# Later values for the large attention units, two gates ahead of the last values, and scores in four PSUM banks

## The chip, the cores and the metric

The kernel runs on one core of a Trainium2 chip. The metric is the device time of one execution in microseconds (us). Lower is better. Six queues of work appear in the profile: PE (TensorE matmuls), PEld (its weight loads), DVE (VectorE), ACT (ScalarE), POOL (GpSimd) and SP (SyncE, which issues the DMAs here).

## The reference

A trunk of two layers over 512 tokens of width 1024. In a layer, x is normalised and projected by one wide matrix into all inputs of two branches. One branch (NSA) has 8 query heads in 2 groups and adds three attentions per head, each with its own gate: over compressed keys, over selected blocks of keys, over a window. With 512 tokens, 8 blocks of 64 and a window of 512, the selection takes every block and the window every earlier token, so the second and the third are plain causal attentions over two sets of keys. The other branch (GLA) is a gated linear attention in chunks of 64. Then

```
y   = sigmoid(p_mg_nsa) * (o_nsa @ w_up_nsa) + sigmoid(p_mg_gla) * (o_gla @ w_up_gla)
out = x + rms(y @ w_out) * g_post
```

## The kernel before

**Precision and weights.** Large products are made of three fp32r matmuls: each operand is split in a rounded part and a rest (`H`, `Lo`), and `split3` adds H·H, H·Lo, Lo·H. Weights come in a fixed order (`ORDER`) through SP into `raw` (3 buffers). ACT makes H (L145) and DVE makes Lo (L146), both into the pool `hl`, whose 6 buffers hold three weights. `get` asks for the weights two places ahead.

**Order of the work.** PE's instructions run in the order in which the program writes them. ACT, DVE, POOL and SP get their order from a planner at build time, which works with its own estimates. Projections are generators in a `queue`: `fill(us)` lets about so many microseconds of queued matmuls out on PE, `need(name)` runs the queue until `name` is done. So the projections of the layer (`q`, `nz`, then for f = 0..7 the gate `mgg` and the up-projection `ug` of the GLA branch) are spread between the steps of the attention.

**The attention.** Heads are worked in four pairs p (heads p and p+4). A pair has five units, so there are 20 units n, with m = n % 5:

- m = 0 is the compressed attention, in three steps: scores into a bank of pool `s`, then softmax; PE transposes of the weights into a bank of pool `t` (L755), which ACT reads (L757) and then DVE (L758); and the product with the compressed values (L761, L762), which opens the pair's accumulator, the only bank of pool `o`.
- m = 1, 2 are the small units (first 256 tokens, key sets 0 and 1). m = 3, 4 are the large units (last 256 tokens, key sets 0 and 1). Each has three steps: `scores` for its first block of 128 tokens, `scores` for its second, and the values (L840), 32 matmuls in each pair of large units, which add to the accumulator. One call of `scores` (at m = 1 it serves both key sets) takes two PSUM banks, one for each head, and PE fills them in that order (L799). DVE reads them (L812), ACT takes the exponential (L814), DVE scales (L816, L817) and transposes in blocks (L778). The result goes out to DRAM (`tp<-T`, L783) and back in another layout (`PT<-tp`, L786). The values read that copy.

`go(n)` runs the next step of unit n. After the last values of a pair the accumulator is scaled by DVE (L845), rounded by ACT (L847), and the rest is made by POOL (L848); that is `oTn[p]`.

**PSUM.** Eight banks: 3 in `mm` (projections), 2 in `s`, 2 in `t`, 1 in `o`.

**After the attention.** For f = 0..7, `up` makes a gate projection `mgn` (24 matmuls) and an up-projection `un` (12 matmuls) over `oTn[0..3]`, three matmuls for each k.

```
        for n in range(len(steps) + 3):
            m = n % 5
            ...
            go(n)
            if m == 2:
                go(n - 4)
                go(n - 3)
```

These two calls are the values of the large units of the pair before. For the last pair they come in the loop's last round, n = 22.

Of the kernel before, what the change touches and what calls it, by code (L numbers as in the profile page):

```python
# [19 lines left out]
KT = D // 128  # L20
# [39 lines left out]
FILL = [(1.6, 1.6, 1.6, 1.6), (1.0, 0.7, 0.9, 1.0), (1.2, 1.0, 1.0, 1.0), (1.5, 1.2, 1.5, 1.8), (1.3, 1.0, 1.0, 1.0)]  # L60
# [4 lines left out]
def trunk(ctx, tc, x, wpk, sp, gvec, cs, wa, out):  # L65
# [23 lines left out]
    def new(pl, shape=(128, 512), dt=F32, tag=None, bufs=None):  # L89
        cnt[0] += 1  # L90
        kw = {} if bufs is None else {"bufs": bufs}
        return sb[pl].tile(list(shape), dt, tag=tag or pl, name=f"{tag or pl}_{cnt[0]}", **kw)

    def ps(tag):
        cnt[0] += 1
        return psp[tag].tile([128, 512], F32, tag=tag, name=f"ps_{tag}_{cnt[0]}")
# [57 lines left out]
    def get(l, n, ahead=2):  # L154
        issue(POS[l, n] + ahead)
        return ready.pop((l, n))

    def split3(o, w, h, first, last):

        mm(o, w[0], h[0], start=first, stop=False)  # L160
        mm(o, w[0], h[1], start=False, stop=False)  # L161
        mm(o, w[1], h[0], start=False, stop=last)  # L162

    def fm(l, n, hT, then):

        w = get(l, n)
        o = ps("mm")
        for k in range(KT):
            if type(w) is list:
                wk = [t[:, k % 4 * 128:(k % 4 + 1) * 128] for t in w[k // 4]]  # L170
            else:
                wk = [t[:, k * 128:(k + 1) * 128] for t in w]
            split3(o, wk, hT(k), k == 0, k == KT - 1)
            if k == KT - 1:
                then(o)
            yield 0.64
# [94 lines left out]
    for l in range(L):  # L271
# [15 lines left out]
        def put(name, gen):  # L287
            queue.append((name, gen))
# [3 lines left out]
        def fill(us):  # L292
            credit[0] += us
            while credit[0] > 0.3 and queue:
                credit[0] -= step(*queue[0])

        def step(name, gen):
            try:
                return next(gen)
            except StopIteration:  # L300
                queue.pop(0)
                done.add(name)
                return 0.0

        def need(name):
            while name not in done:
                step(*queue[0])
# [78 lines left out]
        for t in range(2):  # L386
            o = ps("s")
# [186 lines left out]
        def up(f, gate, wn, src, then):  # L574
            th = []

            def sig(o):
                th.append(new("th"))
                A.activation(th[0], o, AF.Tanh, scale=0.5)

            yield from fm(l, f"{gate}{f}", hT, sig)
            w = get(l, f"{wn}{f}")
            u = ps("mm")
            for k in range(4):
                sl = slice(k * 128, (k + 1) * 128)
                split3(u, (w[0][:, sl], w[1][:, sl]), src[k], k == 0, k == 3)
                if k == 3:
                    then(th[0], u)
                yield 0.64
# [138 lines left out]
        oTn = [None] * 4  # L728
# [33 lines left out]
            mm(acc, vbd[1], pcT, start=False, stop=False, skip_group_check=True)  # L762
            yield

        PT, TT, held, back = {}, {}, {}, []

        def turn(p, br, i, pps):

            ip, n = i // 2, i + 1
            r = (4 * ip + 3) * 64
            if i % 2 == 0:
                TT[p, br] = new("T", (128, 4, r), tag=f"T{ip}")
            T = TT[p, br]
            t = T[:, :, (i % 2) * i * 64:((i % 2) * i + n) * 64].rearrange("p b (j g q) -> p b j g q", j=n, g=2)
            for g in range(2):
                V.transpose(t[:, :, :, g], pps[g][:, :n * 128].rearrange("p (j b q) -> p b j q", j=n, b=4))  # L778
            if i % 2:
                cnt[0] += 1  # L780
                dr = dram.tile([128, 4, r], F32, tag=f"tp{ip}", name=f"tp_{cnt[0]}", bufs=2)
                with tc.issue_after(back[-1]) if back else nullcontext():
                    dma(dr, T)  # L783
                W = PT[p, br, ip] = new("PT", (128, 4, r), tag=f"PT{ip}")
                for b in range(4):
                    back.append(dma(W[b * 32:(b + 1) * 32], dr[:, b].rearrange("(a k) r -> k a r", a=4)).ins)  # L786

        def scores(p, i, brs):

            w = (i + 1) * 128
            ww = w * len(brs)
            both = len(brs) > 1
            o = [ps("s"), ps("s")]
            for g in range(2):
                for n in range(2):
                    kn = first[g][:, n].rearrange("p b n -> p (b n)") if both else keys[brs[0]][g][n][:, :w]
                    mm(o[g][:, :ww], PR[p][1][g][:, i * 128:(i + 1) * 128], kn, start=(n == 0), stop=(n == 1))  # L799
            pps = [weigh(p, g, i, brs, o[g]) for g in range(2)]  # L800
            turn(p, brs[0], i, [t[0] for t in pps])
            if both:
                held[p] = [t[1] for t in pps]

        def weigh(p, g, i, brs, o):
            h, w = p + 4 * g, (i + 1) * 128
            out = []
            for n, br in enumerate(brs):
                ob = o[:, n * w:(n + 1) * w]
                sx = new("sm", (128, 4), tag="sx", bufs=8)  # L810
                pp = new("g")
                V.tensor_tensor_reduce(pp[:, :w], ob, cmask[:, 512 - w:512], 1.0, -3 * NEG,  # L812
                                       OP.add, OP.min, sx[:, 0:1])
                A.activation(pp[:, :w], pp[:, :w], AF.Exp, bias=sx[:, 0:1], scale=-1.0,  # L814
                             accum_out=sx[:, 1:2])
                V.reciprocal(sx[:, 2:3], sx[:, 1:2])  # L816
                V.tensor_scalar(pp[:, :w], pp[:, :w], sx[:, 2:3],  # L817
                                gt[:, i, h * 3 + 1 + br:h * 3 + 2 + br], op0=OP.mult, op1=OP.mult)
                out.append(pp)
            return out  # L820
# [31 lines left out]
        steps = []  # L852
# [5 lines left out]
        def go(n):  # L858
            if 0 <= n < len(steps):
                next(live[n])  # L860


        for n in range(len(steps) + 3):
            m = n % 5
            f4 = FILL[m]
            if n < len(steps):
                if m == 0:
                    need(f"q{steps[n][0]}")
                if m == 4:
                    need(f"nz{steps[n][0]}")  # L870
            go(n)
            if m == 2:
                go(n - 4)
                go(n - 3)
            fill(f4[0])
            if m == 1:
                go(n - 1)
            fill(f4[1])
            if m != 0:
                go(n)  # L880
                fill(f4[2])
            if m == 2:
                go(n - 2)
            if m == 4:
                go(n - 3)
                go(n - 2)
            fill(f4[3])
        need("ug7")

        yT = []  # L890

        def take_un(f):
            def g(th, u):
                t_ = new("p")
                V.scalar_tensor_tensor(t_, th, 1.0, u, op0=OP.add, op1=OP.mult)  # L895
                G.tensor_tensor(t_, t_, y2[f], op=OP.add)  # L896
                if f < 3:
                    both = new("PT", (128, 2, 512), F32R, tag="PT1") if f < 2 else new("T", (128, 2, 512), F32R, tag="T1")
                    H, Lo = both[:, 0], both[:, 1]
                else:  # L900
                    H, Lo = new("g", dt=F32R), new("g", dt=F32R)
                A.mul(H, t_, 0.5)
                V.scalar_tensor_tensor(Lo, t_, 0.5, H.bitcast(F32), op0=OP.mult, op1=OP.subtract)
                yT.append((H, Lo))
            return g

        for f in range(8):
            put(f"un{f}", up(f, "mgn", "un", oTn, take_un(f)))
        need("un7")


# [7 lines left out]
        for s in range(ST):  # L919
# [4 lines left out]
            o = [ps("s" if s % 2 and n < 2 else "mm") for n in range(len(pieces))]  # L924
# [100 lines left out]
```

## Time and profile before

| | |
|---|---|
| median of 3 runs | 850.48 us (849.61 to 852.71) |
| profiled execution, own time | 847.07 us |
| its span in the profile | 845.0 us |
| PE busy | 792.1 us, 94% |
| DVE busy | 560.0 us, 66% |
| ACT, POOL busy | 352.7 us, 94.6 us |

The span lies 2.07 us below the execution's own time. PE is the busiest engine by far. A matmul of 512 columns is listed with some 0.39 us because matmuls overlap, and the next one starts about 0.23 us later, so the busy share is not the share of its peak. Bracketed numbers at the end of a timeline row are the time in which the engine stood idle before that row, and who ended it.

### The profile page before, as it was taken

To read this page: it belongs to the slowest core of one execution; us is meant where nothing else is said; L and a number is where in the kernel's file an instruction comes from. 1 tells how busy PE (TensorE), PEld (TensorE's weight loads), DVE (VectorE), ACT (ScalarE), POOL (GpSimd) and SP (SyncE) were. 2 spreads that over 40 slices of the span, in tenths; PEclk is the share of its full clock that TensorE was granted. 3 is DMA by queue.
4 is the path that set the end of the run, shared out by engine and by line. 5 is a ranking of instruction groups with operands and counts; after the bars stand their busy time and mean duration, and the time that the engine had idled before them with its cause. 6 is when DMAs were issued, how large, how long until landed. Compare 5 with 4: busy or idle time off the path is not lost. (4 is left out here: it accounts for less than half of the span.)

```text
span 845.0 us, 11999 instructions
## 1 busy us (share of the span) xinstructions
PE 792.1 (94%) x4250; PEld 647.3 (77%) x4250; DVE 560.0 (66%) x1272; ACT 352.7 (42%) x727; POOL 94.6 (11%) x118
## 2 busy tenths in 40 slices
PE   3999999999999969999999999998898999799996
PEld 3888788777777748888898878886686777588886
DVE  5653748998978845555564375788987978275322
ACT  4681236554534423442256313555452545154311
POOL 3100023011000001121010001400000000112100
PEclk9999999999999989999999999999999999899999
DMA  8532124367657483546245121434857677355322
GB/s 286 164 125 86 51 67 122 105 183 224 213 165 237 142 233 91 183 138 209 85 136 203 51 75 51 115 91 142 232 175 206 188 206 221 108 152 163 98 100 74
DMA packets 54555, 124.55 MB, mean 147 GB/s; under 512 B 6592, under 2 KB 23520, under 8 KB 54496
## 3 DMA queue, kind: packets, MB, share of 16 engines
q1 hardware_dynamic: 54496, 123.79, 47.5%
q8 instruction: 33, 0.54, 0.3%
q14 instruction: 26, 0.21, 0.1%
HBM read 95.46 MB, written 25.17 MB: 143 GB/s over the span
## 5 line engine op out<-in xcount | busy, mean ns | idle before, releaser
L160 PE MATMUL ps_mm<-hT,hl 128*128 128x512 f32 x544 | 218.9, 402 | 0.0
L161 PE MATMUL ps_mm<-hT,hl 128*128 128x512 f32 x544 | 213.1, 392 | 0.0
L162 PE MATMUL ps_mm<-hT,hl 128*128 128x512 f32 x544 | 212.7, 391 | 0.0
L146 DVE TENSOR_TENSOR hl<-raw,hl 128x1024 fp32r<-128x1024 f32 (+3 forms) x109 | 126.6, 1163 | 48.5 <-ACT hl L145 46.3
L145 ACT CAST hl<-raw 128x1024 fp32r<-128x1024 f32 (+3 forms) x110 | 100.0, 912 | 135.0 <-PE ps_mm L161 95.8
L160 PEld LDWEIGHTS ps_mm<-hT,hl 128*128 128x128 f32 x544 | 102.7, 189 | 24.3 <-issue 4.4
L162 PEld LDWEIGHTS ps_mm<-hT,hl 128*128 128x128 f32 x544 | 102.6, 189 | 22.4
L161 PEld LDWEIGHTS ps_mm<-hT,hl 128*128 128x128 f32 x544 | 102.9, 189 | 18.9
L814 ACT ACTIVATE g<-g,sx 128x128 f32<-128x128 f32 (+3 forms) x128 | 71.1, 556 | 91.7 <-DVE sx L812 90.1
L778 DVE STREAM_TRANSPOSE T<-g 128x256 f32<-128x256 f32 (+3 forms) x128 | 61.2, 497 | 13.2 <-DMA tp<-T 12.6
L812 DVE CUSTOM_DVE_ANT_0 g<-ps_s,cmask 128x128 f32<-128x128 f32 (+3 forms) x128 | 58.2, 476 | 8.4 <-PE ps_s L799 8.1
L840 PE MATMUL ps_o<-PT,a 128*64 128x256 f32 (+1 forms) x384 | 42.9, 368 | 21.3 <-DMA PT<-tp 21.3
L817 DVE TENSOR_SCALAR g<-g,sx,gt 128x128 f32<-128x128 f32 (+3 forms) x128 | 56.6, 454 | 0.9
L840 PEld LDWEIGHTS ps_o<-PT,a 128*64 128x64 f32 x384 | 27.8, 144 | 38.0 <-issue 26.3
L799 PE MATMUL ps_s<-a,a 128*128 128x256 f32 (+2 forms) x224 | 48.3, 334 | 4.9 <-DVE sx L812 4.8
L161 PE MATMUL ps_mm<-oT,hl 128*128 128x512 f32 x128 | 50.0, 391 | 0.0
L160 PE MATMUL ps_mm<-oT,hl 128*128 128x512 f32 x128 | 50.0, 390 | 0.0
L162 PE MATMUL ps_mm<-oT,hl 128*128 128x512 f32 x128 | 49.8, 389 | 0.0
L799 PEld LDWEIGHTS ps_s<-a,a 128*128 128x128 f32 x224 | 37.7, 188 | 13.0 <-DVE sx L812 7.7
L848 POOL TENSOR_TENSOR oT<-p,oT 128x512 fp32r<-128x512 f32 x8 | 10.4, 1296 | 248.1 <-ACT oT L847 248.1
L183 POOL TENSOR_TENSOR rs<-ms,mhalf 128x1 f32<-128x1 f32 (+1 forms) x24 | 18.0, 751 | 174.2 <-DVE ms L181 170.6
L896 POOL TENSOR_TENSOR p<-p,g 128x512 f32<-128x512 f32 x16 | 25.4, 1589 | 107.7 <-DVE p L895 96.2
(250 smaller groups left out, 1263.3 us busy)
## 6 DMA issues: line engine op xcount, KB each, us to landing
raw<-wpk SPq DMA_DIRECT2D x96, 512.0 KB, 3.8
tp<-T SPq DMA_DIRECT2D x16, 896.0 KB, 4.5
PT<-tp SPq DMA_DIRECT2D x64, 224.0 KB, 4.8
raw<-wpk SPq DMA_DIRECT2D x32, 256.0 KB, 3.2
tp<-T SPq DMA_DIRECT2D x16, 384.0 KB, 2.6
PT<-tp SPq DMA_DIRECT2D x64, 96.0 KB, 2.2
a<-wpk SPq DMA_DIRECT2D x16, 256.0 KB, 4.4
p<-x SPq DMA_DIRECT2D x16, 256.0 KB, 2.7
```

What stands on the lines that cost most here:

```text
L145: A.copy(H[:, :w], r[:, :w])
L146: (G if i == 1 else V).tensor_tensor(Lo[:, :w], r[:, :w], H[:, :w].bitcast(F32), op=OP.subtract)
L160: mm(o, w[0], h[0], start=first, stop=False)
L161: mm(o, w[0], h[1], start=False, stop=False)
L162: mm(o, w[1], h[0], start=False, stop=last)
L778: V.transpose(t[:, :, :, g], pps[g][:, :n * 128].rearrange("p (j b q) -> p b j q", j=n, b=4))
L799: mm(o[g][:, :ww], PR[p][1][g][:, i * 128:(i + 1) * 128], kn, start=(n == 0), stop=(n == 1))
L812: V.tensor_tensor_reduce(pp[:, :w], ob, cmask[:, 512 - w:512], 1.0, -3 * NEG, OP.add, OP.min, sx[:, 0:1])
L814: A.activation(pp[:, :w], pp[:, :w], AF.Exp, bias=sx[:, 0:1], scale=-1.0, accum_out=sx[:, 1:2])
L817: V.tensor_scalar(pp[:, :w], pp[:, :w], sx[:, 2:3], gt[:, i, h * 3 + 1 + br:h * 3 + 2 + br], op0=OP.mult, op1=OP.mult)
L840: mm(acc[g * 64:(g + 1) * 64, (i0 + 2) * 128 - w:(i0 + 2) * 128], vsw[j // 2][:, j % 2, c0:c0 + 64], m, start=False, stop=(br == 1 and j = ...
L896: G.tensor_tensor(t_, t_, y2[f], op=OP.add)
```

## The change

Three edits, in the attention of each layer.

1. The values of the large units of a pair move from m = 2 of the next pair to its m = 3. The product that opens the next accumulator moves with them, from m = 2 to m = 3.
2. The loop ends after 20 rounds. For the last pair, the rest of the queue is run first, then the gate projections `mgn0` and `mgn1`, then the values of units 18 and 19, then the rest of `un0`, `un1` and the others.
3. Successive calls of `scores` take their two banks from `s` and `t` in turn, by a counter `nsc` that starts at 0 in each layer. A pair has seven such calls. The transposes L755 stay in `t` and the compressed scores in `s`.

```diff
-        PT, TT, held, back = {}, {}, {}, []
+        PT, TT, held, back, nsc = {}, {}, {}, [], [0]
...
-            o = [ps("s"), ps("s")]
+            nsc[0] += 1
+            o = [ps("ts"[nsc[0] % 2]) for _ in range(2)]
...
-        for n in range(len(steps) + 3):
+        for n in range(len(steps)):
             m = n % 5
             f4 = FILL[m]
...
             go(n)
-            if m == 2:
-                go(n - 4)
-                go(n - 3)
+            if m == 3:
+                go(n - 5)
+                go(n - 4)
             fill(f4[0])
             if m == 1:
                 go(n - 1)
             fill(f4[1])
             if m != 0:
                 go(n)
                 fill(f4[2])
-            if m == 2:
-                go(n - 2)
+            if m == 3:
+                go(n - 3)
             if m == 4:
                 go(n - 3)
                 go(n - 2)
             fill(f4[3])
         need("ug7")
+
+        uns = [up(f, "mgn", "un", oTn, take_un(f)) for f in range(8)]
+        for f in range(2):
+            for k in range(KT):
+                next(uns[f])
+        go(len(steps) - 2)
+        go(len(steps) - 1)
         for f in range(8):
-            put(f"un{f}", up(f, "mgn", "un", oTn, take_un(f)))
+            put(f"un{f}", uns[f])
         need("un7")
```

## Rows read from the trace of the kernel before

**Rows 1.** The page: busy time of each engine over the span

```profile
PE 792.1 (94%) x4250; PEld 647.3 (77%) x4250; DVE 560.0 (66%) x1272; ACT 352.7 (42%) x727; POOL 94.6 (11%) x118
```

**Rows 2.** Waits of PE, whole span: total us, times, longest

```profile
PE ps_o L840 <- DMA PT<-tp: 21.3, 8, 6.6
...
PE ps_s L799 <- DVE sx L812: 4.8, 4, 1.9
PE ps_t L755 <- DVE g L751: 2.7, 3, 0.9
PE ps_t L755 <- ACT g L814: 1.9, 1, 1.9
```

**Rows 3.** Timeline of PE: values of large units, end of the attention

```profile
237.84 1.73 PE L840 MATMUL ps_o<-PT,a 128*64 128x256 f32 x16 [1.84 <-DMA PT<-tp]
...
305.20 1.74 PE L840 MATMUL ps_o<-PT,a 128*64 128x256 f32 x16
313.49 3.20 PE L840 MATMUL ps_o<-PT,a 128*64 128x256 f32 x16 [6.55 <-DMA PT<-tp]
316.62 0.50 PE L160 MATMUL ps_mm<-hT,hl 128*128 128x512 f32 x1
...
322.23 0.39 PE L160 MATMUL ps_mm<-oT,hl 128*128 128x512 f32 x1
322.46 0.39 PE L161 MATMUL ps_mm<-oT,hl 128*128 128x512 f32 x1
...
725.37 3.25 PE L840 MATMUL ps_o<-PT,a 128*64 128x256 f32 x16 [6.33 <-DMA PT<-tp]
```

**Rows 4.** Windows of layer 0: the four pairs, and the very last values

```profile
core 0: us, PE busy (x) PEld busy (x) DVE busy (x) ACT busy (x) POOL busy (x), PEclk, DMA share, GB/s
147.60:181.00 33.40, 30.73 (x148) 24.89 (x146) 32.15 (x94) 18.39 (x45) 2.59 (x2) 1.00 0.38 118
181.00:219.50 38.50, 36.67 (x200) 29.28 (x199) 34.55 (x102) 18.30 (x48) 3.56 (x2) 1.00 0.71 206
219.50:258.20 38.70, 35.97 (x197) 28.71 (x196) 32.50 (x101) 18.24 (x45) 1.30 (x1) 1.00 0.66 201
258.20:296.00 37.80, 36.66 (x200) 29.27 (x199) 31.45 (x97) 16.61 (x44) 1.30 (x1) 1.00 0.65 192
...
313.49:316.69 3.20, 3.20 (x17) 1.97 (x17) 0.00 (x0) 0.00 (x0) 0.00 (x0) 0.53 0.02 5
```

**Rows 5.** Timeline of SP's queue, end of the attention in layer 0

```profile
298.06 1.74 SPq L786 DMA_DIRECT2D PT<-tp  x4
302.36 0.34 SPq L783 DMA_DIRECT2D tp<-T  x1
302.80 1.33 SPq L132 DMA_DIRECT2D raw<-wpk  x2
306.97 1.75 SPq L786 DMA_DIRECT2D PT<-tp  x4
```

**Rows 6.** Timelines of DVE, ACT and POOL, end of the attention

```profile
306.21 1.22 DVE L146 TENSOR_TENSOR hl<-raw,hl 128x1024 fp32r<-128x1024 f32 x1
316.72 0.69 DVE L845 SCALAR_TENSOR_TENSOR p<-ps_o,oT 128x512 f32<-128x512 f32 x1 [9.29 <-PE ps_o L840]
322.90 0.69 DVE L146 TENSOR_TENSOR hl<-raw,hl 128x512 fp32r<-128x512 f32 x1 [5.49 <-ACT hl L145]
...
317.45 0.62 ACT L847 CAST oT<-p 128x512 fp32r<-128x512 f32 x1 [11.28 <-DVE p L845]
...
318.15 1.29 POOL L848 TENSOR_TENSOR oT<-p,oT 128x512 fp32r<-128x512 f32 x1 [35.58 <-ACT oT L847]
```

**Rows 7.** Timeline around L755 and L758, pairs 0 and 2, layer 0

```profile
155.34 0.60 PE L755 MATMUL ps_t<-ident,g 128*64 128x128 f32 x4
156.48 0.63 PE L799 MATMUL ps_s<-a,a 128*128 128x256 f32 x4
157.22 0.58 ACT L757 CAST p<-ps_t 64x512 fp32r<-64x512 f32 x1
159.65 0.68 DVE L758 TENSOR_TENSOR p<-ps_t,p 64x512 fp32r<-64x512 f32 x1
166.62 0.62 PE L799 MATMUL ps_s<-a,a 128*128 128x384 f32 x2 [1.94 <-DVE sx L812]
...
231.65 0.64 PE L799 MATMUL ps_s<-a,a 128*128 128x256 f32 x4
232.72 0.69 DVE L758 TENSOR_TENSOR p<-ps_t,p 64x512 fp32r<-64x512 f32 x1
```

More of the change, by code (lines that the diff above doesn't have):

```diff
@@ L860, in go @@
                 next(live[n])
-        for n in range(len(steps) + 3):
[L864 to L871, printed above, removed]
-            if m == 2:
-                go(n - 4)
-                go(n - 3)
[L875 to L881, printed above, removed]
-            if m == 2:
-                go(n - 2)
[L884 to L888, printed above, removed]
         yT = []
@@ L905, in take_un @@
             return g
+        for n in range(len(steps)):
+            m = n % 5
+            f4 = FILL[m]
+            if m == 0:
+                need(f"q{steps[n][0]}")
+            if m == 4:
+                need(f"nz{steps[n][0]}")
+            go(n)
+            if m == 3:
+                go(n - 5)
+                go(n - 4)
+            fill(f4[0])
+            if m == 1:
+                go(n - 1)
+            fill(f4[1])
+            if m != 0:
+                go(n)
+                fill(f4[2])
+            if m == 3:
+                go(n - 3)
+            if m == 4:
+                go(n - 3)
+                go(n - 2)
+            fill(f4[3])
+        need("ug7")
+        uns = [up(f, "mgn", "un", oTn, take_un(f)) for f in range(8)]
[4 more added lines that the diff above has]
+        go(len(steps) - 1)
         for f in range(8):
-            put(f"un{f}", up(f, "mgn", "un", oTn, take_un(f)))
+            put(f"un{f}", uns[f])
         need("un7")
```

## The prediction

> **What bounds the kernel now.** First the page: PE is busy 94% of the span, the next engine, DVE, 66% [rows 1]. So what PE waits for is what can be won, and work that leaves another engine wins nothing by itself. Then the waits of PE. The largest entry is the values' matmuls waiting for the copy that comes back from DRAM: 21.3 us in 8 waits. Behind it stand 4.8 us in which scores wait for DVE to empty their bank, and 2.7 + 1.9 us in which the transposes L755 wait for the softmax [rows 2]. All three lie in the attention, and the change touches each.
>
> Then the timeline, to see which of the eight waits weigh. In each layer one stands at the very end of the attention: 6.55 us in layer 0, 6.33 us in layer 1 [rows 3]. That is 12.9 us. The other six share 21.3 − 12.9 = 8.4 us. The one shown, at 237.84, is the largest with 1.84 us, and it belongs, as the others do, to the large units of a pair whose values come at m = 2 of the next.
>
> The long waits have a second price. After 6.55 us without work the 16 matmuls of unit 19 take 3.20 us, where the 16 of unit 18 before the wait took 1.74 us [rows 3]. The granted clock of that stretch is 0.53, the lower of the two levels (1.2 of 2.4 GHz) for nearly all of it, where the pairs ahead show 1.00 [rows 4].
>
> SP's queue shows why the end waits. The last block's transposes go out at 302.36, the copy back is issued at 306.97, and PE goes on at 313.49 [rows 5, 3]: 11.1 us for the way through DRAM. The queue of projections ran dry before that: from 305.20 on PE has only values, and the matmuls that follow at 316.62 are already `mgn0` [rows 3]. So the loop's last round finds nothing to put in front of them.
>
> **The end of the attention (edit 2).** It adds no work. It puts `mgn0` and `mgn1` ahead of the two last values. One gate is 24 matmuls, from 316.62 to 322.23: 5.6 us [rows 3]. The GLA work ends at 305.20, as before. The two gates end at 305.2 + 11.2 = 316.4, unit 18 at 318.1, and unit 19 needs a copy that has landed by 313.5. That leaves 4.6 us to spare, so the whole wait goes, and with it the slow clock: 6.55 + 1.46 in layer 0, 6.33 + 1.51 in layer 1, in sum −15.85 us.
>
> Can the gates run that early? The rest of `mgn1` is made by 307.43 [rows 6], and it is wanted at 310.8. `un1` takes the buffers that `mgn0` frees: before, the weight of 512 columns followed the end of a gate at 322.23 by 1.4 us (its rest is done at 323.59 [rows 6]), so it is ready at some 312.2. It is wanted after `un0`, not before 319.8 + 12 × 0.23 = 322.6. `get` now asks for `mgn2` earlier, one 512 KB load further up in SP's queue, but no copy of the attention is issued after it.
>
> What is late next is `oTn[3]`. Before, the 5.6 us of `mgn0` hid it. Now only `un0` stands behind the last values. From the end of unit 19 (313.49 + 3.20 = 316.69) DVE, ACT and POOL need until 319.44, that is 2.75 us [rows 6]. PE has nine matmuls over the first three heads and one on the rounded part of the fourth before it needs the rest: 10 × 0.23 = 2.3 us [rows 3]. So it waits 0.45 us, and behind it waits all of PE. If one rest of 1.22 us [rows 6] stands before it on DVE it is 1.7 us. I take 0.5, twice: +1.0 us, with 0 and +3.4 as bounds.
>
> **Values a step later (edit 1).** The same 32 matmuls, later by the fills of m = 2, nominally 1.2 + 1.0 + 1.0 + 1.0 = 4.2 us of projections, and by the scores of a block. The six waits are at most 1.84 us, so the copies have landed. −8.4 us. The accumulator is freed later too, but the product that opens the next one is moved behind it by the same step, and before its place come two fills of 1.5 and 1.2 us, where the scaling of the old one takes 0.69 us [rows 6]. The buffers of the copies are free before the copy of the next large unit is asked for, since the values still stand ahead of that unit's second scores. Nothing on SP is moved. If DVE, not PE, sets the pace (below), up to all of this comes back.
>
> **Four banks for the scores (edit 3).** A call of scores now waits for the call before the last, so the 4.8 us [rows 2] can go. Two things stand against the full sum. First, the waits lie where DVE is full: in pair 0 it is busy 32.15 of 33.40 us, PE 30.73 [rows 4]. That pair can shrink by 1.25 us in a layer before DVE is the limit, and what PE gains beyond that it would give back at the next transposes L755. I count 2 × 1.25 = −2.5 us, bounds −4.8 and 0.
>
> Second, the scores now share `t` with the transposes. By the counter, the second call of pairs 0 and 2 is even and goes to `t`. It needs both banks there, and it comes right behind L755, which holds one until DVE has done L758. Before, these had nothing to do with each other. In pair 0, L799 starts at 156.48, its second bank at some 156.8, and L758 ends at 160.33: 3.5 us. In pair 2 it is 231.97 against 233.41: 1.4 us [rows 7]. Layer 1 repeats both. PE works in the program's order, so projections queued behind that call wait too. As these rows stand: 2 × (3.5 + 1.4) = +9.8 us. The least is ACT and DVE at once after the transposes: 155.34 + 0.60 + 0.58 + 0.68 = 157.20 [rows 7], 0.4 us each time, +1.6 us. The planner sets DVE's order anew, and with PE held there it has a reason to put L758 forward. I take the wait of pair 2, where ACT and DVE came soon, for all four: 4 × 1.4 = +5.6 us.
>
> On this edit the Trainium skill has a rule: in Perfetto Trace Analysis, section Optimizing Tensor Performance, "Independent matmul groups should rotate through different PSUM banks", so that emptying one overlaps the matmuls of the next. By it the edit gives its 4.8 us and costs nothing. The rows above do not bear that out, since the banks that are added are not unused ones.
>
> **Sum.** −15.85 + 1.0 − 8.4 − 2.5 + 5.6 = −20.15 us. The profiled execution's 847.07 us would become 826.9 us. It lies 3.4 us below the median of the runs, 850.48 us, and the forecast is for the median: 830.3 us.
>
> **The rivals.**
>
> *DVE takes over.* The attention without PE's waits needs more of DVE: in the four pairs of layer 0 it is busy 32.15 + 34.55 + 32.50 + 31.45 = 130.65 of 148.40 us, 88% [rows 4]. If its order leaves no more room, the values' 8.4 us and the scores' 2.5 us come back as waits for DVE at L799 and L755, and the shared bank costs nothing on top. Then only the end is won: −14.85 us, 835.6 us. For it speaks pair 0. Against it: in pairs 1 to 3 DVE is free 4.0 to 6.4 us each.
>
> *The banks pay in full.* The planner puts L758 forward and DVE keeps pace: −15.85 + 1.0 − 8.4 − 4.8 = −28.05 us, 822.4 us. That is also the rule above, taken as it stands.
>
> *The end is not hidden.* If the last copy lands later by more than the 4.6 us to spare, say 8 us because DVE falls behind PE once PE no longer waits, some 4 us of the wait stay in each layer: −12 us, 838 us. Against it: the waits of PE that go in the last pair are some 2 us, less than half of what is to spare.
>
> *Slower.* One mechanism, the shared bank. The planner leaves L758 behind block transposes and rests of weights, and all of PE stands behind the scores in pairs 0 and 2. The other terms give −25.75 us, so at 6.4 us each the four waits use it all up. At 8 us they are 32 us, and the time is 856.7 us. The longest that the rows show is 3.5 us.
>
> **How the numbers follow.** About 0.5%, 4.25 us, is what a measurement here can tell from no change. Chances: the sum above 0.56, DVE takes over 0.20, the banks in full 0.12, the end not hidden 0.05, the slower case 0.07, of which I give 0.03 to a wait that just about uses up the gain and 0.04 to more. Faster 0.93, same 0.03, slower 0.04. For the range I take the bounds: all good, −15.85 + 0 − 8.4 − 4.8 + 1.6 = −27.45 us, 823.0; and on the other side the end with +3.4, half of the values' gain, the bank as its rows stand: −15.85 + 3.4 − 4.2 − 2.5 + 9.8 = −9.35 us, 841.1. This holds the sum, the two likeliest rivals and the unhidden end, save the ends. I give 821 to 840.
>
> **What would show it.** At the end of the attention no wait of PE for the copy, `mgn0` and `mgn1` ahead of the last values, these at 1.74 us per 16 with a clock of 1.00, and a wait of about half a microsecond at the fourth head of `un0`. No waits for the copy at the middle values. The scores' waits on the block before gone, and new ones in pairs 0 and 2 whose releaser is L758 (DVE, or ACT's L757). The prediction is wrong if waits at L755 or L799 grow to the size of what edit 1 wins, if the projections start to wait for weights, or if the last values still stand still.

## The result and the profile after

| | before | after |
|---|---|---|
| median of 4 runs each | 850.70 us | 832.14 us (830.28 to 832.50) |
| profiled execution, own time | 847.07 us | 832.50 us |
| its span | 845.0 us | 830.4 us |

The ratio of the times is 0.9775, 95% interval 0.9751 to 0.9798: 2.25% faster. The forecast was 830.3 us in a range of 821 to 840. By the medians 18.6 us are won, where the sum said 20.15. By the two profiled executions it is 14.6 us, because the one of before lies 3.6 us below its median here (3.4 below the median that the prediction had), and the one of after 0.4 above its own.

In the changed kernel some lines have moved: L799 is now L800, L812 is L813, L840 to L848 are one line further down. The page's first part, which answers to [rows 1], hardly differs. The same work is done on each engine:

```profile
PE 790.9 (95%) x4250; PEld 648.0 (78%) x4250; DVE 557.5 (67%) x1272; ACT 354.4 (43%) x727; POOL 99.5 (12%) x118
```

What differs are the waits. The waits of PE after the change, as in [rows 2] (total us, times, longest):

```profile
PE ps_t L800 <- DVE p L758: 4.7, 2, 2.4
PE ps_t L800 <- DVE sx L813: 4.4, 4, 1.7
PE ps_t L755 <- DVE sx L817: 4.2, 2, 2.1
PE ps_o L841 <- DMA PT<-tp: 1.8, 2, 1.1
PE ps_mm L161 <- POOL oT L849: 1.7, 2, 0.9
```

The 21.3 us for copies have become 1.8 us, and both that are left are at middle values. The scores' waits have grown from 4.8 to 9.1 us. The transposes wait 4.2 us, where it was 4.6. New are 1.7 us at the fourth head of `un0`.

PE's timeline after, first around the scores of pairs 0 to 2 in layer 0, then at a middle value, then at the end of the attention:

```profile
159.03 0.51 PE L800 MATMUL ps_t<-a,a 128*128 128x256 f32 x2 [1.68 <-DVE sx L813]
192.89 0.60 PE L755 MATMUL ps_t<-ident,g 128*64 128x128 f32 x4 [2.09 <-DVE sx L817]
234.97 0.75 PE L800 MATMUL ps_t<-a,a 128*128 128x256 f32 x2 [2.35 <-DVE p L758]
284.15 1.73 PE L841 MATMUL ps_o<-PT,a 128*64 128x256 f32 x16 [1.11 <-DMA PT<-tp]
...
318.60 3.25 PE L841 MATMUL ps_o<-PT,a 128*64 128x256 f32 x32
321.78 0.50 PE L160 MATMUL ps_mm<-oT,hl 128*128 128x512 f32 x1
325.36 0.50 PE L161 MATMUL ps_mm<-oT,hl 128*128 128x512 f32 x1 [0.85 <-POOL oT L849]
```

At the end no wait for the copy is left. All 32 matmuls of units 18 and 19 take 3.25 us together, which is what the 16 of unit 19 alone took before [rows 3]. The clock can be seen in the windows (columns as in [rows 4]): pairs 0, 1 and 2 of layer 0, and 2 us right behind the wait at 234.97:

```profile
148.16:182.31 34.15, 32.48 (x167) 26.59 (x165) 33.33 (x98) 19.54 (x48) 2.58 (x2) 1.00 0.45 138
182.31:223.19 40.88, 38.27 (x201) 30.39 (x201) 35.77 (x101) 19.07 (x46) 2.87 (x2) 0.96 0.64 193
223.19:263.91 40.72, 38.28 (x200) 30.36 (x199) 35.19 (x106) 18.15 (x46) 2.15 (x1) 0.96 0.62 189
...
235.00:237.00 2.00, 2.00 (x6) 1.71 (x7) 1.86 (x5) 0.39 (x1) 0.00 (x0) 0.51 0.15 55
```

In these 2 us PE starts 6 matmuls, some 0.43 us apart, where the same matmuls follow each other by some 0.23 us in stretches at 1.00: the granted clock is 0.51, the lower level for nearly all of it. The windows of layer 1 show 1.00, 1.00 and 0.96 in the same three pairs. A pair of 40.8 us at a mean of 0.96 loses up to 1.6 us, so the three pairs lose up to 4.9 us.

Pair 0 of layer 0 is 1.4 us shorter than it was (a pair runs here from one compressed score to the next, 34.15 us against 35.58), pairs 1 and 2 are 2.3 and 1.3 us longer. The first edit acts in these pairs too; what the third does there is read below, against e1_no_banks.

### The profile page after: what moved, and what is told of

It is laid out like the page before. It is cut to its first block, busy times and chain, and to the rows that moved or that the text cites. A ratio compares the mean times of both kernels' runs of the same rounds, so it can differ in the third digit from the quotient of the medians.

```text
span 830.4 us, 12007 instructions
## 1 busy us (share of the span) xinstructions
PE 790.9 (95%) x4250; PEld 648.0 (78%) x4250; DVE 557.5 (67%) x1272; ACT 354.4 (43%) x727; POOL 99.5 (12%) x118
## 5 line engine op out<-in xcount | busy, mean ns | idle before, releaser
L146 DVE TENSOR_TENSOR hl<-raw,hl 128x1024 fp32r<-128x1024 f32 (+3 forms) x109 | 119.5, 1098 | 52.5 <-ACT hl L145 43.6
L778 DVE STREAM_TRANSPOSE T<-g 128x256 f32<-128x256 f32 (+3 forms) x128 | 58.9, 492 | 0.7
L849 POOL TENSOR_TENSOR oT<-p,oT 128x512 fp32r<-128x512 f32 x8 | 13.6, 1696 | 254.6 <-ACT oT L848 254.6
L841 PE MATMUL ps_o<-PT,a 128*64 128x256 f32 (+1 forms) x384 | 38.6, 348 | 1.8 <-DMA PT<-tp 1.8
L869 POOL TENSOR_TENSOR p<-p,g 128x512 f32<-128x512 f32 x16 | 28.0, 1753 | 84.2 <-DVE p L868 72.7
L841 PEld LDWEIGHTS ps_o<-PT,a 128*64 128x64 f32 x384 | 25.4, 137 | 16.2 <-issue 6.8
L813 DVE CUSTOM_DVE_ANT_0 g<-ps_s,cmask 128x128 f32<-128x128 f32 (+3 forms) x64 | 29.2, 485 | 9.1 <-PE ps_s L800 9.1
L800 PE MATMUL ps_t<-a,a 128*128 128x256 f32 (+2 forms) x112 | 25.1, 337 | 9.1 <-DVE p L758 4.7
L162 PE MATMUL ps_mm<-hl,hT 128*128 128x296 f32 (+1 forms) x96 | 32.4, 338 | 1.4 <-DVE hT L213 1.4
```

The lines of the kernel that those rows point to most:

```text
L146: (G if i == 1 else V).tensor_tensor(Lo[:, :w], r[:, :w], H[:, :w].bitcast(F32), op=OP.subtract)
L841: mm(acc[g * 64:(g + 1) * 64, (i0 + 2) * 128 - w:(i0 + 2) * 128], vsw[j // 2][:, j % 2, c0:c0 + 64], m, start=False, stop=(br == 1 and j = ...
```

## The experiments

Twelve kernels were run in four groups, each group beside the kernel before; a ratio is to the kernel before of its own group. The medians of the kernel before differ between groups (849.95 to 851.14 us), so kernels of different groups are better compared by their ratios; 0.001 is 0.85 us. All do the whole work but e11_no_scaling, whose expectation says what it leaves out.

| kernel | edit against | median us | ratio to before, 95% interval |
|---|---|---|---|
| the change | before | 832.14 | 0.9775 (0.9751 to 0.9798) |
| e1_no_banks | edits 1 and 2 | 826.60 | 0.9720 (0.9700 to 0.9740) |
| e2_only_banks | edit 3 | 846.60 | 0.9962 (0.9944 to 0.9981) |
| e3_only_end | edit 2 | 832.30 | 0.9783 (0.9761 to 0.9805) |
| e4_only_later | edit 1 | 844.37 | 0.9927 (0.9909 to 0.9946) |
| e5_bank_table | the change, other turn of banks | 823.01 | 0.9675 (0.9652 to 0.9699) |
| e6_gate_split | e1, two gate steps last | 824.75 | 0.9700 (0.9676 to 0.9724) |
| e7_table_split | e5 and e6 | 819.44 | 0.9637 (0.9613 to 0.9662) |
| e8_one_gate | e1, one gate ahead | 832.16 | 0.9798 (0.9767 to 0.9830) |
| e9_parity | the change, turn swapped | 828.16 | 0.9748 (0.9721 to 0.9774) |
| e10_cmp_in_t | e7, compressed scores in `t` | 820.89 | 0.9663 (0.9639 to 0.9686) |
| e11_no_scaling | e7, less work on DVE | 815.21 | 0.9602 (0.9573 to 0.9631) |
| e12_copy_first | e7, SP's order held | 920.80 | 1.0849 (1.0810 to 1.0887) |

### The three edits one by one

**Without the third edit** (e1_no_banks).

```diff
-            nsc[0] += 1
-            o = [ps("ts"[nsc[0] % 2]) for _ in range(2)]
+            o = [ps("s"), ps("s")]
```

> The changed kernel without its third edit: every call of scores takes its two banks from pool s, as before the change. My theory: the shared bank costs PE more than the two more banks save. In the traces the waits at the scores went from 4.8 us to 9.1 us, and three stretches at the lower clock follow such waits, some 1.5 us each. So without the edit the time falls below the changed kernel's 832.1 us by 3 to 8 us, to some 826 us, and the scores' waits are back at 5 us or less. Rival, that more banks pay as the rule of rotating banks says: the time rises by some 5 us, to 837 us. Rival, that DVE sets the pace of the attention anyway: 832 us, no difference, the waits only change their place.

826.6 us, 5.5 us below the change by the medians and 4.7 by the ratios, and the intervals of the two don't meet. The third edit costs time here. The scores wait 4.5 us again. Pairs 0 to 2 of layer 0 in this kernel:

```profile
147.58:184.23 36.65, 34.39 (x167) 27.46 (x164) 34.02 (x99) 19.49 (x48) 2.59 (x2) 0.95 0.41 125
184.23:222.59 38.36, 36.46 (x201) 29.09 (x200) 35.34 (x102) 18.71 (x46) 2.84 (x2) 1.00 0.70 209
222.59:260.47 37.88, 36.62 (x200) 29.28 (x200) 34.92 (x105) 18.12 (x46) 1.82 (x1) 1.00 0.66 204
```

Pair by pair the third edit both wins and loses. Against these rows, pair 0 of the changed kernel is 2.5 us shorter, pairs 1 and 2 are 2.5 and 2.8 us longer. In layer 1 it is −2.7, +1.0 and +3.2 us. That is +4.3 us of the 4.5 by which the two spans differ (830.4 and 825.9 us). In pair 0 of both layers the scores' waits of 0.32 and 1.94 us, with the lower clock behind them (0.95 over the pair), have given way to one of 1.7 us.

**The third edit alone** (e2_only_banks, the same lines put into the kernel before).

> The kernel before with the third edit alone: scores alternate between pools s and t, nothing else is changed. My theory: slower than before by 2 to 7 us, 853 to 857 us against 850.7, with new waits at the scores behind L758 in pairs 0 and 2 of each layer. Rival, rotating banks pay: some 846 us. Rival, DVE sets the pace: 850 us.

846.6 us: faster than before by 0.4%, its interval clear of 1. My theory missed the sign. The same waits stand behind the shared bank, but in pair 2 of this kernel they cost nothing (second call of the scores, then the values of pair 1):

```profile
233.26 0.50 PE L800 MATMUL ps_t<-a,a 128*128 128x256 f32 x2 [1.42 <-DVE p L758]
...
237.70 1.74 PE L841 MATMUL ps_o<-PT,a 128*64 128x256 f32 x16 [0.21 <-issue]
```

Where PE stood 1.84 us for the copy before [rows 3], it has now stood 1.42 us for the bank already, and finds the copy there. Two waits in a row for two things that go on at the same time cost the longer one, not the sum. Edit 1 takes the copy's wait away, and then the bank's wait is paid in full. That accounts for pair 2. How the 3.3 us by the medians are made up is not settled, since the two spans differ by 1.0 us only.

**The second edit alone** (e3_only_end). Against the changed kernel:

```diff
-            o = [ps("ts"[nsc[0] % 2]) for _ in range(2)]
+            o = [ps("s"), ps("s")]
...
-            if m == 3:
-                go(n - 5)
-                go(n - 4)
+            if m == 2:
+                go(n - 4)
+                go(n - 3)
...
-            if m == 3:
-                go(n - 3)
+            if m == 2:
+                go(n - 2)
```

> The kernel before with the second edit alone: two gates ahead of the last values, the other large values still at m = 2, scores in pool s. My theory: the end of the attention gives 14.2 us (6.55 + 1.46 + 6.33 + 1.51 less twice 0.85), so 836.5 us. Rival, the end was hidden work that returns later, in the up-projections or in the output stage: 845 us or more.

832.3 us, 17.7 us below the 849.95 us of before in this group and 4.2 us below what I expected. The whole of it stays; nothing comes back in the up-projections or the output stage. This edit alone reaches the time of the whole change: what the first wins and what the third loses nearly cancel.

**The first edit alone** (e4_only_later).

```diff
-        for n in range(len(steps) + 3):
+        for n in range(len(steps) + 4):
...
-            if m == 2:
+            if m == 3:
+                go(n - 5)
                 go(n - 4)
-                go(n - 3)
...
-            if m == 2:
-                go(n - 2)
+            if m == 3:
+                go(n - 3)
```

> The kernel before with the first edit alone: large values and the opening of the next accumulator at m = 3, the last pair's values still at the end of the loop, which is a round longer, scores in pool s. My theory: six waits of 8.4 us in sum go, 842 to 844 us. Rival, DVE sets the pace: the waits come back at L755 or L799, 849 to 851 us.

844.4 us, 5.6 us won, just above the 842 to 844 that I expected. By the medians edits 1 and 2 add up: 17.65 + 5.58 = 23.2 us, and e1_no_banks, which has both, wins 23.35. In the trace of e4_only_later the waits at middle values fall from 8.4 to 2.9 us, but the two at the end grow, from 6.55 and 6.33 to 7.57 and 7.49 us. PE comes to the end of layer 0 sooner and finds that the copy lands when it did (PE goes on at 313.49 in the kernel before):

```profile
313.48 3.25 PE L840 MATMUL ps_o<-PT,a 128*64 128x256 f32 x16 [7.57 <-DMA PT<-tp]
```

So without the second edit layer 0 gives back at its end what it has won. Not all waits for the copy went. In the trace of e1_no_banks four stay at middle values, 4.4 us in sum. SP's queue shows what keeps them, first before the change, then in e1_no_banks, at the last copy of pair 1, layer 0:

```profile
226.11 0.34 SPq L783 DMA_DIRECT2D tp<-T  x1
226.54 1.44 SPq L132 DMA_DIRECT2D raw<-wpk  x2
230.75 1.75 SPq L786 DMA_DIRECT2D PT<-tp  x4
```

```profile
227.87 0.34 SPq L783 DMA_DIRECT2D tp<-T  x1
228.77 7.07 SPq L132 DMA_DIRECT2D raw<-wpk  x2
235.94 1.79 SPq L786 DMA_DIRECT2D PT<-tp  x4
```

Both times two weight loads stand between the way out and the way back. Before, they took 1.4 us, and the copy went 4.6 us after the way out. Now the second load goes out only when DVE has made the rest of an earlier weight,

```profile
234.25 1.22 DVE L146 TENSOR_TENSOR hl<-raw,hl 128x1024 fp32r<-128x1024 f32 x1
```

and the copy behind it goes after 8.1 us. The profile puts the load's wait down to DVE; that it waits for a buffer of `raw` is read from the program, where L146 is the last to read one. From the issue of this copy to PE's going on it takes nearly the same time in both kernels, 7.1 us before (237.84) and 7.2 here (243.10), so the added 3.4 us lie in SP's queue. The copies come later too, and eat part of the step that the values were given.

### The shared bank

**Another turn of the banks** (e5_bank_table).

```diff
-            o = [ps("ts"[nsc[0] % 2]) for _ in range(2)]
+            o = [ps("ssststs"[(nsc[0] - 1) % 7]) for _ in range(2)]
```

> The changed kernel, but the seven calls of scores in a pair take s, s, s, t, s, t, s, the same in each pair. So no call comes to pool t between the transposes L755 and the end of L758, and L755 finds t empty. My theory: what edit 3 costs is the shared bank in pairs 0 to 2, and what it wins is the wait of 2.3 us at the fourth call of pair 0 in each layer with the slow clock behind it. So the time is at or below that of the kernel without the third edit, 820 to 826.6 us, with no wait of scores or L755 behind L758 or behind scores. Rival, the win at pair 0 comes back at L755 in pair 1, since DVE is full there: 826 to 828 us. Rival, two more banks cost in themselves: 832 us.

823.0 us, 9.1 us below the change and 3.6 below e1_no_banks by the medians, 8.5 and 3.8 by the ratios. The interval ends just below that of e1_no_banks (0.9699 against 0.9700). So the two banks do pay, if the call right behind L755 does not come to `t`. One call still meets the bank of L755, which I had not expected: the fourth of pair 1, in each layer. L758 ends at 200.64 there, nine us behind its transposes.

```profile
200.79 0.59 PE L800 MATMUL ps_t<-a,a 128*128 128x384 f32 x2 [0.54 <-DVE p L758]
```

Its windows of pairs 0 and 1 in layer 0:

```profile
147.66:179.86 32.20, 32.20 (x166) 26.52 (x164) 31.34 (x94) 18.22 (x45) 2.59 (x2) 1.00 0.40 122
179.86:220.20 40.34, 36.90 (x200) 29.12 (x200) 37.32 (x110) 20.32 (x50) 2.81 (x2) 1.00 0.71 216
```

In pair 0 PE has not one gap, and DVE is busy 31.34 of 32.20 us. Pair 1 is 2.0 us longer than the 38.36 us of e1_no_banks, with waits for DVE at its first scores (1.77 us) and at L755 (1.13 us). Part of the win of pair 0, 4.45 us against e1_no_banks, comes back there, as the rival said.

**The turn swapped** (e9_parity): `"st"` for `"ts"`.

> The changed kernel with the turn of the two pools swapped: the first call of scores in a layer takes t, the second s. So the second call, which follows the transposes L755, takes t in pairs 1 and 3 instead of 0 and 2. My theory: the waits behind the shared bank move with it; the second calls of pairs 0 and 2 (1.7 and 2.35 us) wait no more, those of pairs 1 and 3 do, by 1 to 2.5 us. The time stays within 4 us of 832.1. Rival, DVE is simply full in pairs 0 and 2: waits of about the same size stay in these pairs.

828.2 us, 4 us below the change by the medians; the intervals of the two overlap. Pairs 0 lose their waits (32.20 us each), and at the scores of pair 2 none is left. Pair 3 now has one, where the changed kernel had none. Pair 1 waits 0.53 us, less than I expected, and for its own first bank:

```profile
193.91 0.51 PE L800 MATMUL ps_t<-a,a 128*128 128x256 f32 x2 [0.53 <-DVE sx L813]
269.98 0.50 PE L800 MATMUL ps_t<-a,a 128*128 128x256 f32 x2 [1.85 <-DVE p L758]
```

The wait follows the bank, not the pair; its length differs from pair to pair.

**The compressed scores in `t`** (e10_cmp_in_t).

```diff
-            c = ps("s")[:, 0:256]
+            c = ps("t")[:, 0:256]
```

> The fastest kernel so far (bank table and gate split) with the compressed scores in pool t instead of s. There the first scores of pair 1 wait 1.77 us in each layer for DVE to empty the bank of the compressed scores (L743). If that wait is one for a bank, it goes: 819.4 less 3.5 us, 816 us. Rival, which I hold more likely now: DVE is full in pairs 0 and 1 (31.3 of 32.2 and 37.3 of 40.3 us), so the wait moves to L755 in the same pair, which needs the same softmax: 819 us.

820.9 us, no gain: the intervals of the two overlap. The wait moved. In e7_table_split pair 1 waits at the scores and at L755, here at L755 alone, for as long:

```profile
188.94 0.47 PE L800 MATMUL ps_s<-a,a 128*128 128x256 f32 x2 [1.77 <-DVE g L743]
191.93 0.60 PE L755 MATMUL ps_t<-ident,g 128*64 128x128 f32 x4 [1.13 <-ACT g L815]
```

```profile
191.76 0.60 PE L755 MATMUL ps_t<-ident,g 128*64 128x128 f32 x4 [2.97 <-DVE g L751]
```

**Less work on DVE** (e11_no_scaling).

```diff
-                V.tensor_scalar(pp[:, :w], pp[:, :w], sx[:, 2:3],
-                                gt[:, i, h * 3 + 1 + br:h * 3 + 2 + br], op0=OP.mult, op1=OP.mult)
```

> The fastest kernel so far (bank table and gate split) without the scaling of the softmax weights by gate and sum (one DVE instruction of some 0.47 us for each block and head, 128 in all); the attention's output is not normalised. It bounds what DVE's load still costs. If DVE sets the pace in pairs 0 and 1, the waits for DVE at scores and L755 (6.9 us in sum) go, and most of the waits for copies (3.5 us) as well: 809 to 814 us. Rival, DVE's load is no matter by now and these waits are of banks and order: 817 to 820 us.

815.2 us, 4.2 us less than e7_table_split by the medians and 3.0 by the ratios, between my theory and the rival. The intervals of the ratios overlap, the times themselves do not. The spans differ by 4.4 us (817.6 and 813.2). Pairs 0 and 1 of layer 0 without the scaling:

```profile
148.22:180.43 32.21, 32.21 (x167) 26.52 (x165) 28.66 (x86) 19.12 (x48) 2.60 (x2) 1.00 0.49 153
180.43:218.61 38.18, 36.66 (x200) 29.05 (x199) 30.57 (x87) 19.99 (x48) 3.82 (x2) 1.00 0.66 202
```

Pair 0 is as long as in e7_table_split (32.20 us), where PE has no gap. Pair 1 is 2.15 us shorter (40.33 there); DVE's busy time in it falls from 37.30 to 30.57 us, and of the 3.4 us of waits 1.5 are left. The waits for copies stay at 3.3 us. So DVE's load costs PE time in pair 1, some 2 us in each layer, and the copies wait for something else.

### The end of the attention

**Two gate steps behind the last values** (e6_gate_split), and **with the table of banks** (e7_table_split).

```diff
-        for f in range(2):
-            for k in range(KT):
+        for f, n in ((0, KT), (1, KT - 2)):
+            for k in range(n):
                 next(uns[f])
         go(len(steps) - 2)
         go(len(steps) - 1)
+        for k in range(2):
+            next(uns[1])
```

> The changed kernel without the third edit, and the last two of the eight steps of the gate mgn1 (6 matmuls, 1.4 us) run behind the last values instead of ahead of them. My theory: they cover the 0.84 us that un0 waits in each layer for the rest of its fourth head, and the last copy has landed 1.4 us earlier too: 826.6 less 1.7 us, 825 us. Rival, the copy lands late: no gain, waits for the copy at the last values.

> Both of the two edits above together, on the changed kernel. My theory: their gains add, 818.5 to 825 us, and it is the fastest of all kernels here.

824.75 and 819.44 us: 1.85 us below e1_no_banks, and 3.6 below e5_bank_table. Neither difference is clear of its intervals. In the traces of both the wait at the fourth head is gone (0.84 and 0.85 us in each layer without the split), and no wait for a copy has come at the end. By the medians e7_table_split is the fastest kernel here that does all of the work.

**One gate ahead** (e8_one_gate).

```diff
-        for f in range(2):
+        for f in range(1):
```

> The changed kernel without the third edit, with only mgn0 ahead of the last values (mgn1 runs after un0). It tries the spare time that the prediction gave as 4.6 us: with 5.6 us less in front, PE should wait about 1 to 2 us for the last copy in each layer, and the wait at the fourth head of un0 stays. My theory: 828 to 831 us. Rival, one gate is enough and the second one hides nothing: 826.6 us.

832.2 us, 5.6 us more than e1_no_banks by the medians, and more than I expected. With 5.6 us less in front PE waits again, 2.94 us in layer 0 and 2.98 in layer 1, and the lower clock is back with it:

```profile
313.92 3.25 PE L840 MATMUL ps_o<-PT,a 128*64 128x256 f32 x16 [2.94 <-DMA PT<-tp]
```

So the spare time of e1_no_banks was some 5.6 − 2.94 = 2.7 us, if the copy lands at the same time in both; it was issued 0.4 us later here. The second gate is needed.

**The copy first in SP's queue** (e12_copy_first).

```diff
-        dma(r[:, :w], src)
+        with tc.issue_after(lastb[-1]) if lastb else nullcontext():
+            dma(r[:, :w], src)
...
+                lastb.append(back[-1])
```

> The fastest kernel so far (bank table and gate split), with SP's order held: a weight load that the program asks for after a copy back (PT<-tp) is also issued after it. In the kernels with the first edit SP issues two weight loads between a pair's last tp<-T and its PT<-tp, the second waits for its buffer, and the copy goes out 8 us after the tp<-T where it was 4.6 us before the edit. My theory: that is why two to four waits for the copy stay at the middle values (3.5 us here). With the copy first they go, 816 us. Rival, the loads then come late and PE waits for weights instead: 819 to 830 us, with waits of PE at the projections.

920.8 us. The rival was right, and far beyond its numbers. No wait for a copy is left, but the projections wait for their weights (waits of PE):

```profile
PE ps_mm L162 <- ACT hl L147: 69.6, 22, 6.3
...
PE ps_mm L164 <- DVE hl L148: 5.0, 7, 1.4
```

In that kernel PE is so much later everywhere that the missing waits for copies prove nothing. That the loads ahead of the copy keep the 2 to 4 middle waits alive is read from SP's rows, and no run shows it by itself.

## Why the prediction was right

Its likeliest case came about: the end gives most, the later values less, and the shared bank takes some back. That 18.6 us came so near to 20.15 is in part luck. Run one by one, the end won 2.8 us more than forecast and the later values 2.8 us less, and the banks cost 1.6 us more. Step by step:

**The end.** Predicted −15.85 + 1.0 us. In the traces it is −15.85 + 1.7: the waits and the slow clock are gone, and `un0` waits 0.85 us in each layer where I took 0.5. The reason was in the bounds: DVE did a rest and two parts of the output weights first and came to the scaling of the accumulator some 0.8 us late (it starts at 322.62, the values end at 321.85). e3_only_end shows 17.65 us by the medians, 2.8 more than the forecast for this edit, but 14.9 us by the spans of the two traces, which is the forecast. The difference nearly matches the 2.9 us by which the profiled execution of before lies below the median of this group. The runs show in part where that comes from: slower executions of the kernel before have a lower mean clock. In the group of e3_only_end they go from 846.65 us at 0.991 to 852.59 us at 0.984, and e3_only_end has 0.993 to 0.996. Which waits cost the clock in the slower ones is not shown, since no trace of one is there.

**The time to spare** was given as 4.6 us and came out as some 2.7 (e8_one_gate). The copy is behind loads in SP's queue at the end too: in e1_no_banks it goes out 7.0 us after the way out at 299.64, where it was 4.6 us [rows 5]. It sufficed.

**Values a step later.** Predicted −8.4 us, measured −5.6 (e4_only_later, with the longer waits at the end in it). In the changed kernel the middle waits lose 6.6 of their 8.4 us. The step that failed is "Nothing on SP is moved". The program's order of DMAs did not change, but in SP's rows loads that wait now stand longer in front of the copies, and the waits that are left follow from that as far as the rows show it. Of the rival that DVE would take all of it back, e4_only_later leaves nothing.

**Four banks.** Predicted −2.5 + 5.6 = +3.1 us, measured +4.7 by the ratios and +5.5 by the medians (the change against e1_no_banks). The sign was right for the edit beside the other two, and wrong for the edit alone (e2_only_banks). The mechanism, a wait for L758 in the shared bank, came about in pairs 2 only:

- The second calls of pairs 0 wait 1.7 us, near the 1.4 that I took, but for another reason. DVE's timeline of the changed kernel shows it (first the reading of that call's first bank, then L758):

```profile
158.55 0.42 DVE L813 CUSTOM_DVE_ANT_0 g<-ps_t,cmask 128x256 f32<-128x256 f32 x1
...
160.14 0.69 DVE L758 TENSOR_TENSOR p<-ps_t,p 64x512 fp32r<-64x512 f32 x1
```

  PE went on at 159.03, ahead of L758. The call did not get the bank of L755 at all. Its second head took the bank of its own first head, as soon as that was read. I had counted on its needing both banks. In pairs 0 its own first bank came free first, in pairs 2 that of L755 (L758 ends at 234.91, the first head is read from 236.09), and each time PE went on with that one.
- In pairs 2 the wait is 2.35 us, for L758 as predicted, longer than the 1.4.
- The slow clock behind waits of some 2 us in the middle of the attention was not in the sum at all. It lost up to 4.9 us in three pairs after, and up to 36.66 × 0.05 = 1.8 us in the one pair of layer 1 that had it before:

```profile
556.76:593.42 36.66, 34.48 (x166) 27.50 (x163) 33.77 (x98) 19.70 (x48) 2.59 (x2) 0.95 0.39 121
```

  So +3.1 us at most, about what is missing: the waits alone give −15.85 + 1.7 − 6.6 (copies at the middle) + 4.3 (scores) − 0.4 (L755) = −16.85 us, with the clock −13.75, and the spans differ by 14.6.
- Against e1_no_banks, in the traces, the waits at the scores are 4.6 us longer and those at L755 0.5 us, and the waits for copies are 2.6 us shorter. The clock costs up to 4.9 us in three pairs, where it costs up to 1.8 us in each of the two pairs 0 there. That is up to +3.7 us, and the spans differ by 4.5. Neither the copies nor the clock had a term in the forecast of this edit.

**The rule of the Trainium skill** (Perfetto Trace Analysis, Optimizing Tensor Performance) that groups should rotate through different banks would have given −4.8 us. The runs agree with it where the banks were mostly free: −3.8 us by the ratios from e1_no_banks to e5_bank_table. They disagree where the rotation ran into a bank in use: +4.7 us by the ratios.

**The signs that were named.** The copy's wait at the end, the slow clock there and the waits for L758 in pairs 2 came out as said. Two waits for the copy at middle values stayed, the scores still wait 4.4 us for the reading of a block (L813), and the wait at the fourth head was 0.85 us.

## What to carry to other kernels

A wait at the end of a stage is worth more than its length, if PE comes out of it at the lower clock: 6.55 us of waiting cost 1.46 more here. Independent work of the next stage, put ahead of the last step that waits, won both. More banks help only if they are free at that point of the order, so before sharing a pool look up what else holds a bank there and until when. Waits that follow each other can hide one another, so the price of an edit is to be tried together with the edits that it will stand with: the banks won 3.3 us alone and lost 4.7 (by the ratios) with the others.

## What the runs showed of the hardware

PE fell to the lower clock after short waits too, not only after the long one at the end. After the wait of 2.35 us at 234.97 the granted clock was 0.51 over the next 2 us. After one of 1.42 us, in pair 2 of e2_only_banks, the mean over the pair stayed at 1.00. A wait of 2.09 us at L755 was followed by slow matmuls in layer 0 of the changed kernel (0.96 over the pair) and by none at the same place in layer 1 (1.00). In the kernel before, the scores of pair 0 wait 1.94 us in layer 0 [rows 7] and 1.95 us in layer 1, and the mean over the pair is 1.00 and 0.95. So in these traces the same wait did or did not cost the clock, and a forecast could only bound it.
